# A mixture-of-experts loop: units of 64 slots for a pair of experts, one branch per pair, half of the sums kept in PSUM

## Chip, cores, metric

One core of one Trainium2 chip runs the whole program. The metric is the device time of one execution in microseconds (us); lower is better. Profiles are single executions recorded by the hardware profiler; times of runs are taken without it.

## What is computed

Two layers of a backbone over 512 tokens of width 1024. Each layer has a mixer (latent attention and a convolution in the first, a gated MLP in the second) and then a mixture of experts. The change is in the mixture alone. Cut to it, the reference reads:

```python
def hier_moe(h, w_group, b_group, w_router, b_router, w_gate, w_up, w_down):
    """Top-1 expert group (weight = group softmax prob), then top-2 experts within it."""
    ...
    out = jnp.zeros_like(t)
    for e in range(N_EXPERTS):                      # 32 experts, each 1024 -> 256 -> 1024
        he = (jax.nn.silu(t @ w_gate[e]) * (t @ w_up[e])) @ w_down[e]
        out = out + dense_w[:, e:e + 1] * he        # at most two experts of a token weigh more than 0
    return out.reshape(shp)
...
        h2 = modulate(rms_norm(x, norm2_g[l]), sh2, sc2)
        x = x + g2 * hier_moe(h2, *moe_args)
```

512 tokens with two experts each make 1024 rows for 32 experts, 32 on average. By the reference on its inputs the counts (expert p, expert p + 16) are, for p = 0 to 15:

| layer | counts |
|---|---|
| 0 | (27,35) (26,33) (24,32) (24,34) (17,11) (17,50) (20,19) (15,38) (50,29) (40,20) (36,50) (27,32) (69,42) (42,17) (39,28) (49,32) |
| 1 | (8,10) (39,7) (14,13) (20,2) (33,4) (16,6) (43,9) (23,7) (23,23) (20,103) (14,86) (8,103) (13,69) (42,82) (14,44) (30,96) |

## The kernel before

The kernel sorts the 1024 rows by expert on the chip. `Route` (lines 120 to 292) works out each row's rank within its expert, the experts' counts and where each expert's rows start. The rows of the normed activations are gathered in that order and turned, so that `m.xs` holds them with the channels on the partitions; this row stage also runs the first pair's unit beside it (tables `AUX` and `FIRST` say behind which block of rows what is issued).

`experts` then loops over 16 pairs: step j takes p = 0, 8, 1, 9, ..., 7, 15, that is the experts p and p + 16. A pair has six weight tiles of 1 MB, four with gate and up projections and two with down projections, 96 a layer; they are loaded in that order by SP's queue. About 14 are on their way before the loop, and `st.emit(6, j)` behind pair j's work issues six more.

The common unit holds up to 64 tokens of both experts. `gate_up` (L357) makes 32 matmuls of 512 columns, each with 64 columns of the array for one of the two experts; `act` multiplies silu(gate) by up (ACT L362, DVE L363); `turn` transposes (L370) and copies (ACT L371); `down` (L430) makes 16 matmuls of 512 into two banks. `weighed` multiplies by the token's weight and the layer's gain (DVE L419) and splits the product into a high part (ACT L420) and the rest (DVE L421), since the sums that follow run in a format that rounds; L388 and L389 build the one-hot matrix that says which row of x each slot belongs to. Those sums are sixteen matmuls L400, for four tiles of tokens, two halves of the width, high and rest. Each finished half is added to x at once, six by DVE (L413) and two by ACT and POOL (L410, L411).

`first(j + 1)` runs the next pair's gates and the sums of the pair that is due, between gates and transposes. It stands in both sides of a branch `few` (L623): where no expert of the pair has more than 64 tokens, `first` follows. Otherwise a second pass `again` follows (L451 gates, L459 down) for 64 slots of the expert with more (the `If` at L597 picks which). Behind it a branch `both` (L639) skips the part for pairs in which both experts have more than 64, or one more than 128; that part has a loop with a count in a register (L610). On these inputs it is never entered. Branches of `few` and `both` have a hint (L480, L482) that TensorE's queue issues ahead of them, from the count in a register.

Engines follow their own queues, and the order in each is the order of the code. Waits between them are semaphores.

Of the kernel before, what the change touches and what calls it, by code (L numbers as in the profile page):

```python
# [17 lines left out]
P = 128  # L18
# [3 lines left out]
SLOT = 64  # L22

# [93 lines left out]
class Route:  # L117
# [37 lines left out]
    def end(self, res):  # L155
# [23 lines left out]
        R0 = k.work.tile([P, 8, 64], BF16, name="R0", tag="w2", bufs=NW2)  # L179
# [6 lines left out]
        v.tensor_tensor(R0, io(8, 64), fb[:, 0][:, :, None].to_broadcast([P, 8, 64]), op=OP.is_equal)  # L186
        for q in range(8):
            for e in range(2):
                nc.tensor.matmul(p0[64 * e:64 * e + 64, 0:2], R0[:, q], B0[:, q, e], start=(q == 0), stop=(q == 7))
# [12 lines left out]
        with nc.allow_low_precision(reason="whole numbers under 512"):  # L202
            v.tensor_reduce(res.g0, p0[:, 0:2], axis=AX.X, op=OP.add)
# [10 lines left out]
        pin(v.tensor_copy(it[:, 0], ro[:, 0]))  # L214
# [8 lines left out]
    def starts(self, res):  # L223

        k, cc = self.k, self.cc
        v = k.nc.vector
        cm = k.small.tile([P, 16], F32, name="cm", tag="cm")
        for r in range(8):
            v.tensor_scalar(res.start[:, r], cc[:, 32:64], float(SLOT * r), 1024.0 - SLOT, op0=OP.add, op1=OP.min)
        v.tensor_tensor(cm, cc[:, 0:16], cc[:, 16:32], op=OP.max)  # L230
        v.tensor_copy(res.cnt[:, 0, :], cm)
        res.most = k.work.tile([P, 1], I32, name="most", tag="most")
        v.tensor_reduce(res.most, cm, axis=AX.X, op=OP.max)
        v.tensor_scalar(cc[:, 0:32], cc[:, 0:32], float(SLOT), None, op0=OP.is_gt)
        v.scalar_tensor_tensor(res.cnt[:, 2, :], cc[:, 16:32], 2.0, cc[:, 0:16], op0=OP.mult, op1=OP.add)
        v.tensor_scalar(cc[:, 0:16], cm, 2.0 * SLOT, None, op0=OP.is_gt)
        v.scalar_tensor_tensor(res.cnt[:, 3, :], res.cnt[:, 2, :], 3.0, cc[:, 0:16], op0=OP.is_equal, op1=OP.max)
        v.tensor_scalar(cm, cm, float(SLOT - 1), None, op0=OP.add)
        v.tensor_copy(res.cnt[:, 1, :], cm)
        v.tensor_scalar(res.cnt[:, 1, :], res.cnt[:, 1, :], 6, None, op0=OP.arith_shift_right)  # L240

        d = k.small.tile([P, 2, 16], F32, name="d", tag="rd")
        v.tensor_scalar(d[:, 0], res.cnt[:, 2, :], 2.0, None, op0=OP.is_equal)
        v.tensor_tensor(d[:, 1], res.start[:, 1, 16:32], res.start[:, 1, 0:16], op=OP.subtract)
        v.tensor_tensor(d[:, 1], d[:, 1], d[:, 0], op=OP.mult)
        v.tensor_tensor(res.second, d[:, 1], res.start[:, 1, 0:16], op=OP.add)
# [27 lines left out]
    def columns(self, r):  # L274
# [5 lines left out]
        if r:  # L280
            f = k.small.tile([P, 8], F32, name="fr", tag="fr")
            v.tensor_scalar(f, self.ft[:, 3], -32.0 * r, None, op0=OP.add)
# [51 lines left out]
def moe_bufs(k):  # L334

    m = K()
    ps = [k.psum.tile([P, 512], F32, name=f"mps{i}", tag=f"mps{i}", bufs=1) for i in range(8)]
    m.pg, m.ph, m.py, m.po = ps[0], ps[1], ps[2:4], ps[4:8]
    m.xT = k.work.tile([P, 8, P], F32, name="xT", tag="xT")
    m.mix = k.work.tile([P, D], F32, name="mix", tag="mix")  # L340
    m.xr = m.mix[:, 0:512].rearrange("p (c s) -> p c s", c=8)
    m.sg, m.h = m.mix[:, 512:768], m.mix[:, 768:1024]
    m.row = [k.work.tile([P, D], F32, name=f"row{i}", tag=f"y{i}") for i in range(2)]
    m.g2 = k.work.tile([P, D], F32, name="g2", tag="g2")
    m.hT = m.sg.rearrange("p (f s) -> p f s", f=2)
    m.xs = [W(k, [P, 2, D], "xs") for _ in range(4)]
    m.ic = k.small.tile([P, 2], I32, name="ic", tag="ic")
    m.t4 = k.small.tile([P, NT], F32, name="t4", tag="t4")
    m.tw = k.small.tile([P, 2, 2], F32, name="tw", tag="tw")
# [3 lines left out]
def gate_up(k, m, st, p, cs):  # L353

    for c in cs:
        for h in range(2):
            k.nc.tensor.matmul(m.pg[64 * h:64 * h + 64, :], m.xT[:, c, 64 * h:64 * h + 64], st.gu(p, h, c), start=(c == 0), stop=(c == 7))  # L357


def act(k, m):  # L360

    k.nc.scalar.activation(m.sg, m.pg[:, 0:256], AF.Silu)  # L362
    k.nc.vector.tensor_tensor(m.h, m.sg, m.pg[:, 256:512], op=OP.mult)  # L363


def turn(k, m, n=P):

    nc = k.nc
    for f in range(2):
        nc.tensor.transpose(m.ph[:, f * P:f * P + n], m.h[0:n, f * P:(f + 1) * P], k.ident[0:n, 0:n])  # L370
    nc.scalar.copy(m.hT[:, :, 0:n], m.ph[:, 0:2 * P].rearrange("p (f s) -> p f s", f=2)[:, :, 0:n])  # L371


SIDE = [(0, 1), (2, 0)]
SIDE0 = ()


class Outs:
# [3 lines left out]
    def __init__(self, oh, y):  # L382
        self.oh, self.y = oh, y
        self.left = ()

    def where(self, k, m, tok):
        eng = k.nc.vector
        eng.tensor_scalar(m.t4, k.noff, tok, None, op0=OP.add)  # L388
        eng.tensor_tensor(self.oh.rearrange("p (i t) -> p i t", i=NT), k.iota[:, None, :].to_broadcast([P, NT, P]),  # L389
                                m.t4[:, :, None].to_broadcast([P, NT, P]), op=OP.is_equal)  # L390

    def add(self, k, m, X, tiles):

        for i in tiles:
            for n in range(2):
                self.add_half(k, m, X, i, n)

    def sum_half(self, k, po, i, n, start=True, stop=True):
        for y in self.y:
            k.nc.tensor.matmul(po, self.oh[:, i * P:i * P + P], y[:, 512 * n:512 * n + 512],  # L400
                               start=start and y is self.y[0], stop=stop and y is self.y[-1])

    def add_half(self, k, m, X, i, n, side=SIDE):
        c = slice(512 * n, 512 * n + 512)
        po = m.po[(2 * i + n) % 4]
        if (i, n) in self.left:
            m.one.sum_half(k, po, i, n, stop=False)
        self.sum_half(k, po, i, n, (i, n) not in self.left)
        if (i, n) in side:
            k.nc.scalar.copy(m.tmp, po)  # L410
            k.nc.gpsimd.tensor_tensor(X[i][:, c], X[i][:, c], m.tmp, op=OP.add)  # L411
            return
        k.nc.vector.tensor_tensor(X[i][:, c], X[i][:, c], po, op=OP.add)  # L413


def weigh(k, m, py, w, s, c, hi, lo):

    nc = k.nc
    nc.vector.scalar_tensor_tensor(py[s], py[s], w[s], m.g2[s, c], op0=OP.mult, op1=OP.mult)  # L419
    nc.scalar.copy(hi, py[s])  # L420
    return lambda: nc.vector.tensor_tensor(lo, py[s], hi.bitcast(F32), op=OP.subtract)  # L421


def down(k, m, st, p):

    nc = k.nc
    for n in range(2):
        for f in range(2):
            for h in range(2):
                nc.tensor.matmul(m.py[n][64 * h:64 * h + 64, :], m.hT[:, f, 64 * h:64 * h + 64],  # L430
                                 st.dn(p, h, f)[:, 512 * n:512 * n + 512], start=(f == 0), stop=(f == 1))


def weighed(k, m, w, tok):

    m.one.where(k, m, tok)
    parts = []
    for n in range(2):
        c = slice(512 * n, 512 * n + 512)
        parts.append(weigh(k, m, m.py[n], w, slice(0, P), c, *(y[:, c] for y in m.one.y)))  # L440
    for low in parts:
        low()


def again(k, m, st, p, h, w, tok, fill):

    nc = k.nc
    a, b = slice(0, 64), slice(64, P)
    for c in range(8):
        for q, s in enumerate((a, b)):  # L450
            nc.tensor.matmul(m.ph[s, 256:512], m.xr[:, c], st.gu(p, h, c)[:, 256 * q:256 * q + 256], start=(c == 0), stop=(c == 7))  # L451
    nc.scalar.activation(m.sg[a], m.ph[a, 256:512], AF.Silu)
    nc.vector.tensor_tensor(m.h[a], m.sg[a], m.ph[b, 256:512], op=OP.mult)
    fill(0)
    turn(k, m, 64)
    fill(1)
    for f in range(2):
        for q, s in enumerate((a, b)):
            nc.tensor.matmul(m.py[1][s, :], m.hT[:, f, 0:64], st.dn(p, h, f)[:, 512 * q:512 * q + 512], start=(f == 0), stop=(f == 1))  # L459
    m.two.where(k, m, tok)  # L460
    parts = []
    for q, (s, o) in enumerate(((a, b), (b, a))):
        c = slice(512 * q, 512 * q + 512)
# [1290 lines left out]
```

## Time and profile before

| | us |
|---|---|
| runs, median of 3 | 1421.14 (1418.04 to 1421.16) |
| profiled execution | 1433.02 |
| its span, first to last instruction | 1431.2 |
| first loop over pairs (layer 0) | 242.3 |
| second loop over pairs (layer 1) | 297.8 |

Busy over the span: TensorE 1288.0 us (90%), its weight loads 835.3, DVE 850.7, ACT 558.8, POOL 319.0. The mean granted TensorE clock is 0.951 of full speed. The terms: PE is TensorE, PEld its weight loads, PEq and PEldq their sequencers, DVE, ACT, POOL and SP the others. A row of the chain or of a timeline begins with the start and the length in us. "x32" is a count of instructions. "[1.99 <-PEq L480]" is idle time ahead of the row and what ended it.

### The profile page before, as it was taken

The page shows a single profiled execution, that of the slowest core. Times are in us where ns is not written, and L with a number is a line of the kernel's source. Part 1 is how long each engine was busy: PE and PEld are TensorE (multiplying, and loading weights), DVE is VectorE, ACT ScalarE, POOL GpSimd, SP SyncE. Part 2 cuts the span into 40 slices and gives each one's busy share as a digit, 9 for nine tenths or more (in the row PEclk, how much of TensorE's full clock was granted, in tenths as well). Part 3 has the DMA queues.
Part 4 walks back from the last instruction along what each step waited for, and adds up shares of the span by engine and source line. Part 5 has one row for each costly group of instructions (what it writes and reads, how often), then busy time and mean ns, then how long its engine had stood idle before and what let it go on. Part 6 is the DMA issues. An engine that isn't in the chain of part 4 may idle for free. (4 is left out here: it accounts for less than half of the span.)

```text
span 1431.2 us, 20527 instructions
## 1 busy us (share of the span) xinstructions
PE 1288.0 (90%) x7174; PEld 835.3 (58%) x7174; DVE 850.7 (59%) x1730; ACT 558.8 (39%) x1315; POOL 319.0 (22%) x289
## 2 busy tenths in 40 slices
PE   5999878899996989989969999999995999999997
PEld 3678754454774444444458898997873444444443
DVE  2334687889667546564684455676347566555554
ACT  3244544476444424333352233344324433332331
POOL 0033454587102112121230001220002022111210
PEclk9999988899997999999989999999997999999998
DMA  9411044726546789989856354353367687877771
GB/s 360 156 32 44 17 167 135 293 72 221 221 166 248 287 345 412 413 348 387 354 181 224 123 203 159 133 196 133 122 253 272 261 359 310 344 293 291 297 306 61
DMA packets 54570, 329.12 MB, mean 230 GB/s; under 512 B 8030, under 2 KB 8286, under 8 KB 19634
## 3 DMA queue, kind: packets, MB, share of 16 engines
q1 hardware_dynamic: 48658, 306.29, 55.3%
q0 software_dynamic: 5664, 19.93, 4.3%
q8 instruction: 106, 1.74, 0.5%
q14 instruction: 142, 1.16, 0.2%
HBM read 317.77 MB, written 8.43 MB: 228 GB/s over the span
## 5 line engine op out<-in xcount | busy, mean ns | idle before, releaser
L357 PE MATMUL mps<-w,xT 128*64 128x512 f32 x1024 | 245.2, 632 | 27.6 <-PEq L480 10.1
L357 PEld LDWEIGHTS mps<-w,xT 128*64 128x64 f32 x1024 | 90.3, 145 | 175.9 <-issue 171.0
L411 POOL TENSOR_TENSOR X<-X,tmp 128x512 f32<-128x512 f32 x72 | 92.9, 1291 | 443.1 <-ACT tmp L410 386.4
L700 PE MATMUL ps_c<-wch,hxh 128*128 128x256 f32 x512 | 147.6, 288 | 2.0 <-ACT hxh L706 2.0
L702 PE MATMUL ps_c<-wch,hxl 128*128 128x256 f32 x512 | 145.8, 285 | 1.5 <-DVE rm_m L98 0.9
L701 PE MATMUL ps_c<-wcl,hxh 128*128 128x256 f32 x512 | 146.0, 286 | 0.0
L400 PE MATMUL mps<-oy,ooh 128*128 128x512 f32 x512 | 138.8, 408 | 1.7 <-ACTq L623 1.7
L413 DVE TENSOR_TENSOR X<-X,mps 128x512 f32<-128x512 f32 x206 | 132.8, 683 | 10.8 <-PE mps L400 9.0
L363 DVE TENSOR_TENSOR mix<-mix,mps 128x256 f32<-128x256 f32 x32 | 13.5, 421 | 185.6 <-ACT mix L362 185.6
L430 PE MATMUL mps<-w,mix 128*64 128x512 f32 x512 | 116.9, 598 | 0.0
L400 PEld LDWEIGHTS mps<-oy,ooh 128*128 128x128 f32 x512 | 91.4, 189 | 43.0 <-issue 22.2
L891 POOL TENSOR_TENSOR acc<-acc,ctp 128x497 f32<-128x497 f32 (+14 forms) x71 | 101.8, 1462 | 32.9 <-ACT ctp L890 32.9
L700 PEld LDWEIGHTS ps_c<-wch,hxh 128*128 128x128 f32 x512 | 98.9, 193 | 7.8 <-issue 4.2
L701 PEld LDWEIGHTS ps_c<-wcl,hxh 128*128 128x128 f32 x512 | 99.0, 193 | 4.2 <-issue 3.4
L702 PEld LDWEIGHTS ps_c<-wch,hxl 128*128 128x128 f32 x512 | 98.8, 193 | 4.5 <-issue 1.7
L362 ACT ACTIVATE mix<-mps 128x256 f32<-128x256 f32 x32 | 12.3, 384 | 202.5 <-PE mps L357 199.7
L430 PEld LDWEIGHTS mps<-w,mix 128*64 128x64 f32 x512 | 33.9, 136 | 66.1 <-issue 55.2
L700 PE MATMUL ps_o<-woh,yTh 128*128 128x512 f32 x160 | 64.7, 406 | 2.1 <-ACT v L1333 1.2
L420 ACT CAST oy<-mps 128x512 fp32r<-128x512 f32 x64 | 37.2, 585 | 75.0 <-DVE mps L419 75.0
L706 POOL TENSOR_TENSOR vs<-v,vs 128x512 fp32r<-128x512 f32 x16 | 23.0, 1440 | 182.1 <-ACT vs L706 174.7
L701 PE MATMUL ps_o<-wol,yTh 128*128 128x512 f32 x160 | 63.3, 396 | 0.0
L702 PE MATMUL ps_o<-woh,yTl 128*128 128x512 f32 x160 | 62.9, 394 | 0.0
(412 smaller groups left out, 2527.7 us busy)
## 6 DMA issues: line engine op xcount, KB each, us to landing
w<-in_w_gu_dram SPq DMA_DIRECT2D x128, 1024.0 KB
w<-in_w_down_dram SPq DMA_DIRECT2D x64, 1024.0 KB
wada<-in_w_ada_dram SPq DMA_DIRECT2D x48, 1024.0 KB
wc<-in_c_w_in_dram SPq DMA_DIRECT2D x16, 1024.0 KB
wo<-in_c_w_out_dram SPq DMA_DIRECT2D x8, 1024.0 KB
X<-in_x_dram SPq DMA_DIRECT2D x4, 1024.0 KB
wo<-in_ab_w_out_dram SPq DMA_DIRECT2D x4, 1024.0 KB
h2d<-row POOLq DMA_DIRECT2D x16, 256.0 KB, 5.2
```

Of the source, the lines that this page charges most:

```text
L357: k.nc.tensor.matmul(m.pg[64 * h:64 * h + 64, :], m.xT[:, c, 64 * h:64 * h + 64], st.gu(p, h, c), start=(c == 0), stop=(c == 7))
L363: k.nc.vector.tensor_tensor(m.h, m.sg, m.pg[:, 256:512], op=OP.mult)
L400: k.nc.tensor.matmul(po, self.oh[:, i * P:i * P + P], y[:, 512 * n:512 * n + 512], start=start and y is self.y[0], stop=stop and y is self ...
L411: k.nc.gpsimd.tensor_tensor(X[i][:, c], X[i][:, c], m.tmp, op=OP.add)
L413: k.nc.vector.tensor_tensor(X[i][:, c], X[i][:, c], po, op=OP.add)
L420: nc.scalar.copy(hi, py[s])
L430: nc.tensor.matmul(m.py[n][64 * h:64 * h + 64, :], m.hT[:, f, 64 * h:64 * h + 64], st.dn(p, h, f)[:, 512 * n:512 * n + 512], start=(f == 0 ...
L700: k.nc.tensor.matmul(out, lh, rh, start=start, stop=False)
L701: k.nc.tensor.matmul(out, lh, rl, start=False, stop=False)
L702: k.nc.tensor.matmul(out, ll, rh, start=False, stop=stop)
L706: for i in (k.nc.scalar.copy(hi, src), (eng or k.nc.vector).tensor_tensor(lo, src, hi.bitcast(F32), op=OP.subtract)):
L891: nc.gpsimd.tensor_tensor(d, d, tp, op=OP.add)
```

## The change

A unit now has 64 slots: either 32 tokens of each expert of a pair, or 64 of one. `Unit` (new) has both kinds. For a pair, the array's columns are cut into four groups of 32: expert, and half of the 512 columns (gate or up; left or right half of the down product). For one expert they are two groups of 64, as in the second pass before. Gates, transposes and down products share two banks (`m.pg`, `m.py`).

The sums are eight matmuls, since the high part and the rest lie in one tile `y`, one above the other. The left half of the width (n = 0) is summed in four banks `m.acc` over the whole layer and added to x at its end. The right half goes to two banks and is added by DVE at once, as before; no sum goes by ACT and POOL.

The branches: after a pair's unit, `some(extra)` skips to the join where no expert of the pair has over 32 tokens. Otherwise a unit of one expert follows, and `some(more)` skips what is for still more; that goes through `further`, a loop `For_i` over the number of windows left, which sets the tokens and weights of its window by eight small matmuls. `weigh` of a unit is issued behind the join, or ahead of the next unit of the same pair. The next pair's unit is written once, behind the join, and not in both sides of a branch.

In the row stage the first unit has half of the columns, `Route.heads` makes 32 small matmuls for the tables of the 32-token heads, and the conditional block at L563 is gone. The diff, cut:

```diff
+HEAD = 32
...
+    def heads(self, pt):
+
+        for q in range(8):
+            s = self.S[:, q // 4, q % 4].rearrange("p (a b s) -> p a b s", a=2, b=2)[:, 0, 1]
+            for a in range(4):
+                self.k.nc.tensor.matmul(pt[HEAD * a:HEAD * a + HEAD], s, self.C[q // 4][:, q % 4, :, 0:32], start=(q == 0), stop=(q == 7))
...
-    m.pg, m.ph, m.py, m.po = ps[0], ps[1], ps[2:4], ps[4:8]
...
+    m.pg = ps[7][:, 0:256]
+    m.py, m.po, m.acc = ps[0], ps[1:3], ps[3:7]
...
+            self.parts = [(slice(HEAD * q, HEAD * q + HEAD), slice(HEAD * (q % 2), HEAD * (q % 2) + HEAD), q % 2, q // 2) for q in range(4)]
+            self.x = m.xT
+        else:
+            self.parts = [(s, A, h, q) for q, s in enumerate((A, B))]
+            self.x = m.xr
+
+    def gates(self, cs=range(8)):
+        for c in cs:
+            for r, s, h, q in self.parts:
+                self.k.nc.tensor.matmul(self.m.pg[r], self.x[:, c, s], self.st.gu(self.p, h, c)[:, 256 * q:256 * q + 256], start=(c == 0), stop=(c == 7))
...
+def weigh(k, m):
+
+    v, y, c = k.nc.vector, m.y, [slice(0, 512), slice(512, D)]
+    v.scalar_tensor_tensor(m.py, m.py, m.tw[:, 1:2], m.g2h, op0=OP.mult, op1=OP.mult)
+    for s, cs in zip((A, B), c):
+        k.nc.scalar.copy(y[s, cs], m.py[s])
+    v.tensor_scalar(m.oh, m.seq, m.tw[:, 0:1], None, op0=OP.is_equal)
+    for s, o, cs in zip((A, B), (B, A), c):
+        v.tensor_tensor(y[o, cs], m.py[s], y[s, cs].bitcast(F32), op=OP.subtract)
...
+    def run(u, tw, turned=None):
+
+        u.gates()
+        u.act()
+        for i in range(4):
+            scatter(k, m, m.acc[i], i, 0, False, False)
+        u.turn()
+        for f in range(2):
+            for i in range(2):
+                scatter(k, m, m.po[i], 2 * f + i, 1, True, True)
+                add(m.po[i], 2 * f + i, 1)
+            if turned and f == 0:
+                turned()
+            u.down([f])
+        nc.vector.tensor_copy(m.tw, tw)
+
+    def further(u, h, p, n):
...
+        with tc.For_i(0, n, 1):
+            v.tensor_scalar(m.ic, m.at, float(-HEAD), 1024.0 - SLOT, op0=OP.add, op1=OP.min)
+            window(m.xr, m.ic[0:1])
+            weigh(k, m)
...
+            for q in range(8):
+                nc.tensor.matmul(m.pg[:, 0:2], rt.S[:, q // 4, q % 4], m.cw[:, q], start=(q == 0), stop=(q == 7))
+            v.tensor_copy(m.pw, m.pg[:, 0:2])
+            run(u, m.pw)
...
-        few = tc.If(count(0, p, 512) <= SLOT, preferred_fallthrough_block=False, label=f"few{l}_{j}")
-        with few as more:
-            if not last:
-                first(j + 1, m.one)
...
+        kind = value(0, p, 3)
+        with some(f"extra{l}_{j}", kind):
+            ahead_of(f"more{l}_{j}", 3, p, 16)
+            weigh(k, m)
+            with tc.If(kind == 2) as other:
+                run(us[1], res.tw1[:, :, p + 16])
             with other.Else():
...
+                run(us[0], res.tw1[:, :, p])
+            with some(f"more{l}_{j}", value(3, p, 16)):
+                for h in range(2):
+                    n = value(1 + h, p, 8)
+                    with tc.If(n > 0):
+                        further(us[h], h, p, n)
+        weigh(k, m)
         st.emit(6, j)
```

On TensorE, before, a second pass ends so: the last down matmuls, the jump out of the `If`, the load of the count and the branch `both`, then sums that were left (`oy` and `ooh` are the weighed rows and the one-hot matrix).

```order
L459 MATMUL mps_3750<-w,mix 64x512 x3
L597 UNCONDITIONAL_BRANCH
L473 TENSOR_LOAD cnt
L639 COMPARE_AND_BRANCH
L400 MATMUL mps_3752<-oy_4103,ooh 128x512
L400 MATMUL mps_3752<-oy_4104,ooh 128x512
```

On TensorE, after, a pair's unit ends so: the last down matmuls (32 rows a group), the load of the count and the branch `extra`, the hint for `more`, the `If` on which expert, then a unit of one expert.

```order
L411 MATMUL mps_3746<-w,mix 32x512 x4
L434 TENSOR_LOAD cnt
L444 COMPARE_AND_BRANCH
L434 TENSOR_LOAD cnt [waits DVE_49]
L439 REGISTER_ALU
L1691 BRANCH_PREFETCH_HINT
L596 COMPARE_AND_BRANCH
L392 MATMUL mps_3753<-w,xr 64x256 x16
```

No sum stands behind the branch any more, and a further unit is reached over two branches.

On TensorE, after, the same unit of one expert ends, and `further` follows (L603 the `If` around it, L570 its loop, L579 the small matmuls):

```order
L411 MATMUL mps_3746<-w,mix 64x512 x2
L596 UNCONDITIONAL_BRANCH
L434 TENSOR_LOAD cnt
L444 COMPARE_AND_BRANCH
L434 TENSOR_LOAD cnt
L603 COMPARE_AND_BRANCH
L570 COMPARE_AND_BRANCH
L570 UNCONDITIONAL_BRANCH [waits PE_49]
L570 UNCONDITIONAL_BRANCH [waits barrier_Pool_Activation_PE_DVE_SP_release]
L1691 BRANCH_PREFETCH_HINT
L579 MATMUL mps_3753<-cw,S 128x2 [waits DVE_49]
L579 MATMUL mps_3753<-cw,S 128x2 x7
```

Between two units there stand five branches, a barrier of all engines, and small matmuls that wait for DVE. A second barrier, at the loop's end, waits for the transfer queues too.

On DVE, before, the weighing stands ahead of the branch `few`:

```order
L388 TENSOR_SCALAR t_3765<-ct,tok_102 128x4 [waits DVE_49]
L389 TENSOR_TENSOR ooh<-ct,t_3765 128x512 [waits DVE_49]
L419 SCALAR_TENSOR_TENSOR mps_3749<-mps_3749,w_103,g_3759 128x512 [waits DMASW2_49]
L419 SCALAR_TENSOR_TENSOR mps_3750<-mps_3750,w_103,g_3759 128x512
L421 TENSOR_TENSOR oy_4104<-mps_3749,oy_4103 128x512 [waits DMASW1_49,Activation_49]
L421 TENSOR_TENSOR oy_4104<-mps_3750,oy_4103 128x512 [waits Activation_49]
L473 TENSOR_LOAD cnt
L623 COMPARE_AND_BRANCH
```

On DVE, after, the branch `extra` stands ahead of it (L563 copies the unit's tokens and weights):

```order
L563 COPY tw<-tw_103 128x2 [waits DVE_49]
L434 TENSOR_LOAD cnt
L444 COMPARE_AND_BRANCH
L416 SCALAR_TENSOR_TENSOR mps_3746<-mps_3746,tw,g_3759 128x512 [waits DVE_49,PE_49]
L419 TENSOR_SCALAR oh<-g_3759,tw 128x512
L421 TENSOR_TENSOR y<-mps_3746,y 64x512 [waits DVE_49,Activation_49]
L421 TENSOR_TENSOR y<-mps_3746,y 64x512
L596 COMPARE_AND_BRANCH
```

The load of the count and the branch moved ahead of the weighing, which has one product where it had two.

## Rows read from the trace of the kernel before

**Rows 1.** Busy time by stretch: row stage, layer 0, layer 1, one full stretch.
```profile
core 0: us, PE busy (x) PEld busy (x) DVE busy (x) ACT busy (x) POOL busy (x), PEclk, DMA share, GB/s
444.00:474.60 30.60, 25.52 (x138) 14.05 (x138) 21.03 (x82) 18.30 (x50) 7.61 (x9) 0.89 0.58 191
474.60:716.90 242.30, 234.53 (x1040) 108.57 (x1040) 136.98 (x208) 85.56 (x275) 41.16 (x32) 0.97 0.92 372
1120.30:1418.10 297.80, 279.90 (x1296) 132.89 (x1296) 163.11 (x253) 98.68 (x302) 51.78 (x40) 0.97 0.74 292
540.00:600.00 60.00, 60.00 (x274) 26.38 (x272) 36.66 (x55) 22.29 (x74) 11.12 (x9) 1.00 1.01 412
```
**Rows 2.** The chain that ended last, a pair without a second pass.
```profile
1377.66 6.87 PE mps L357 x32
...
1388.67 3.58 PE mps L430 x16
```
**Rows 3.** The same chain, the second pass of the last pair.
```profile
1408.60 3.67 PE mps L451 x32
1412.28 2.07 PE mps L400 x8
1414.35 0.26 PE mps L370 x2
1414.61 1.59 PE mps L400 x6
1416.20 1.89 PE mps L459 x8
```
**Rows 4.** TensorE's timeline, another stage: matmuls with 32 columns each.
```profile
203.99 1.07 PE L720 MATMUL ps_ada<-wada,sc 128*32 128x512 f32 x8
```
**Rows 5.** TensorE's waits over the span: total us, times, longest us.
```profile
PE mps L357 <- PEq L480: 10.1, 6, 2.3
PE mps L357 <- ACT oy L420: 8.6, 4, 2.2
```
**Rows 6.** TensorE's branches: duration in ns, least, median, greatest; first and last start.
```profile
L639 PEldq COMPARE_BRANCH  x10: 194/280/2891, 1172.2 to 1343.3; - x10
...
L623 PEldq COMPARE_BRANCH  x39: 82/363/6427, 473.4 to 1403.6; - x39
```
**Rows 7.** Busy time by stretch, columns as in rows 1: gates behind two joins.
```profile
1175.30:1182.50 7.20, 7.15 (x33) 2.44 (x34) 2.15 (x3) 0.84 (x2) 0.00 (x0) 1.00 0.96 374
1215.00:1224.00 9.00, 8.92 (x33) 2.94 (x34) 1.69 (x3) 0.62 (x2) 0.00 (x0) 0.81 0.96 391
```
**Rows 8.** The chain that ended last, weighing of the last second pass.
```profile
1418.12 0.76 DVE mps L419
...
1418.90 0.59 ACT oS L420
...
1420.32 0.59 ACT oS L420
...
1420.93 0.70 DVE oS L421
```
**Rows 9.** SP's semaphore steps at the program's end, as in rows 6.
```profile
L1750 SPq EVENT_SEMAPHORE  x14: 17/28/28, 1427.8 to 1431.1; - x14
```
**Rows 10.** DVE's timeline: a small instruction.
```profile
1211.40 0.22 DVE L388 TENSOR_SCALAR t<-ct,tok 128x4 f32<-128x4 f32 x1
```
**Rows 11.** TensorE's timeline in the row stage of layer 0.
```profile
446.65 5.74 PE L357 MATMUL mps<-w,xT 128*64 128x512 f32 x16
...
457.95 3.65 PE L357 MATMUL mps<-w,xT 128*64 128x512 f32 x16
...
462.47 1.95 PE L292 MATMUL mps<-C,S 128*128 128x128 f32 x16
...
467.55 3.65 PE L430 MATMUL mps<-w,mix 128*64 128x512 f32 x16
```

More of the change, by code (lines that the diff above doesn't have):

```diff
@@ L225, in starts @@
         k, cc = self.k, self.cc
[L226 to L233, printed above, removed]
@@ L242, in starts @@
[L242 to L246, printed above, removed]
+        v, sm = k.nc.vector, k.small
+        n, e = sm.tile([P, 4, 16], F32, name="cm", tag="cm"), lambda h: slice(16 * h, 16 * h + 16)
@@ L337, in moe_bufs @@
     ps = [k.psum.tile([P, 512], F32, name=f"mps{i}", tag=f"mps{i}", bufs=1) for i in range(8)]
[L338 to L342 removed]
+    m.pg = ps[7][:, 0:256]
+    m.py, m.po, m.acc = ps[0], ps[1:3], ps[3:7]
+    m.last = m.po + [m.py, m.acc[0]]
@@ L366, in turn @@
[L366 to L413, printed above, removed]
@@ L434, in weighed @@
[L434 to L463, printed above, removed]
-        parts.append(weigh(k, m, m.py[1], w, s, c, m.two.y[0][s, c], m.two.y[0][o, c]))
-    for low in parts:
-        low()
@@ L484, in window, with ahead_of, some @@
-    def window(x, at, act=False):
+                              skip_runtime_bounds_check_because="numbers of windows of at most 512 tokens", **kw)
+    def ahead_of(label, row, p, most):
+        tc.mark_branch_hint_location(label, hint=value(row, p, most, engines=(PE,)) > 0, engines=(PE,))
+    @contextmanager
+    def some(label, v):
+        with tc.If(v <= 0, preferred_fallthrough_block=False, label=label) as g:
+            pass
+        with g.Else():
+            yield
+    def window(x, at, n=SLOT, act=True):
@@ L492, in windows, with heads, seconds @@
-    def windows(j):
+            (nc.scalar.copy if act else nc.vector.tensor_copy)(x[:, 2 * c:2 * c + 2], m.xs[c][:, :, bass.ds(o, n)])
+    def heads(j):
         p = pair(j)
         for h in range(2):
-            window(m.xT[:, :, 64 * h:64 * h + 64], res.start[0:1, 0, p + 16 * h:p + 16 * h + 1], True)
+            e = p + 16 * h
+            window(m.xT[:, :, HEAD * h:HEAD * h + HEAD], res.start[0:1, 0, e:e + 1], HEAD)
+    def seconds(j):
+        p = pair(j)
+        window(m.xr, res.second[0:1, p:p + 1])
@@ L570, in experts @@
-    m.one = Outs(tile([P, 512], "oh"), [tile([P, D], f"y{i}") for i in range(2)])
-    m.two = Outs(tile([P, 512], "C0"), [tile([P, D], "S")])
-    m.tmp = k.work.tile([P, 512], F32, name="tmp", tag="C1")
-    def first(j, due):
-        ahead_of(f"few{l}_{j}", 0, pair(j), 512, SLOT)
-        gate_up(k, m, st, pair(j), range(8))
-        act(k, m)
-        due.add(k, m, X, (0, 1))
-        turn(k, m)
-        if j < 15:
-            windows(j + 1)
-        due.add(k, m, X, (2, 3))
-    ends = [(n, i) for n in range(2) for i in range(4)]
+                ahead_of(f"extra{l}_0", 0, pair(0), 3)
@@ L586, in experts @@
     for j in range(16):
         p = pair(j)
-        last = j == 15
-        window(m.xr, res.second[0:1, p:p + 1], True)
-        ahead_of(f"few{l}_{j}", 0, p, 512, SLOT)
+        seconds(j)
         if j:
-            down(k, m, st, p)
-        weighed(k, m, res.w0[:, p:p + 1], res.tok0[:, p:p + 1])
-        one = lambda r, e: (res.w[:, r, e:e + 1], res.tok[:, r, e:e + 1])
-        def second(fill):
-            with tc.If(count(2, p, 3) == 2) as other:
-                again(k, m, st, p, 1, *one(1, p + 16), fill)
-            with other.Else():
-                again(k, m, st, p, 0, *one(1, p), fill)
@@ L1468 @@
 ROWAHEAD = 0
-FILL = [[(0, 0), (0, 1), (1, 0)], [(1, 1), (2, 0)]]
-LEFT = [(i, n) for i in range(4) for n in range(2) if (i, n) not in FILL[0] + FILL[1]]
 COLWAIT = 3
```

282 lines of the change are left out of this document (129 added, 153 removed).

## The prediction

> **What bounds the kernel now.** I read the table by stage first. The two loops over the pairs of experts take 242.3 and 297.8 us, 540.1 of the span of 1431.2, and TensorE is busy for 234.5 and 279.9 of it [rows 1]. The weights' loads are the other candidate: 96 tiles of 1 MB a layer, and the stretch in which the transfer engines are always busy shows 412 GB/s, so 2.55 us a tile and 245 us a layer; the loops show a share of 0.92 and 0.74 [rows 1]. So TensorE sets the pace, with the loads close behind in layer 0. Then the chain that ended last: a pair without a second pass is nothing but TensorE, 6.87 for the gates, 3.58 for the down products [rows 2] and sixteen sums between them, about 14.6 in all. A second pass costs 3.67 + 2.07 + 0.26 + 1.59 + 1.89 [rows 3]. What TensorE loses, 25.7 us over both loops, lies at branches [rows 5].
>
> **What is counted.** How many tokens each expert has follows from the reference on its inputs. Before, a pair has a second pass where an expert has over 64 tokens: one in layer 0, six in layer 1. Now the common unit holds 32 + 32 slots. In layer 0, 12 of 16 pairs need more than that, in layer 1 ten; of these 22, five need still more: (36, 50) and (69, 42) in layer 0, (20, 103), (8, 103) and (42, 82) in layer 1. Units: 16 + 14 and 16 + 13, 59; the first of each layer runs in the row stage, so 57 run in the loops.
>
> **The unit.** A unit of one expert has the matmuls of today's second pass: 32 of 256 columns, 3.67; two transposes, 0.26; eight of 512, 1.89 [rows 3]. A unit of a pair has the same columns in four groups of 32. Four groups of 32 columns run at once in this kernel: eight matmuls of 512 took 1.07, as two at 0.5 each would [rows 4]. So I give both units the same price. The sums become 8 where the common pass had 16, 0.261 each (2.07 and 1.59 for 14, [rows 3]), 2.09. Unit: 3.67 + 2.09 + 0.26 + 1.89 = 7.91; 57 units, **450.9**. The weighing hides: one DVE product, two ACT copies, one subtraction follow each other, 0.76 + 0.59 + 0.59 + 0.70 = 2.6 [rows 8], with some 0.5 for the branch ahead of them, behind the next gates of 3.67. If that cover were gone, it would be up to 3.1 a unit; I take 0.
>
> **The joins.** Today six joins after a second pass hold TensorE 10.1 us in all, 1.7 each, and four where the `few` branch jumps the other way than the hint had it 8.6 [rows 5]. The branch itself lasts 0.28 in the middle case and 2.89 in the worst [rows 6]. Now: ten pairs without a further unit, one jump each, 1.2 (between 0.3 and 2.2), **12.0**. Fifteen joins behind a second unit with another unit to come, 1.7 each, **25.5** (4 to 43). Entering the 22 further units, 0.2 each, a little under the middle branch of 0.28 [rows 6] (0 to 1.2), **4.4**. After about half of today's joins the granted clock falls: 0.81 over one next pair's gates against 1.00 over another's, where the stretch was 9.0 us for the matmuls that otherwise take 7.2 [rows 7], 1.7 us. Half of fifteen, **12.8** (0 to 25).
>
> **The five loops.** A third window goes through `further`, a loop with a count in a register. Its beginning and its end make every engine wait for every other and for every transfer queue; today's program has that nowhere in the loops (the like loop of before is never entered). Nothing in the trace shows its price, so I build it up. The loads of its counts and branches around it, like a join and a bit: 1.9. A barrier at the entry, 1.0, and one with the queues at the end, 1.6: together 2.6, under the 3.3 in which the program itself closes, from the first to the last of its semaphore steps [rows 9]. Between them nothing overlaps: the weighing, 2.6 [rows 8], four small DVE instructions at 0.22 each [rows 10], eight tiny matmuls into the gates' bank and a copy, 0.9 (the two transposes took 0.26, [rows 3]), 4.4 in all. Back to the next unit 1.9. Sum 10.8, and two stretches at the lower clock, 3.4 [rows 7]: 14.2. Five, **71**. The bounds lie far apart: a join's price, 2.55, from below; three jumps at the worst of today's, 6.43 [rows 6], with 5.7 for the rest, 25, from above. I take the middle, since the serial parts have rows of their own.
> Then the loads. They are queued two to three pairs ahead, and the barrier waits for those on their way. Carried forward pair by pair (6 tiles of 2.55 arrive against 9.1 us of a pair with one unit and 19 of one with two, 14 tiles ahead at the start), some 8.5, 2.2, 6, 2.2 and 0 us are outstanding at the five: **19** (0 to 40).
>
> **Other engines.** On DVE the weighing now stands behind the branch's register load; queued behind it are the next unit's product of the gates and the sums, which come 3.7 us later. Its additions fall from six a unit to four, so DVE has room. ACT and POOL lose the two sums that went by them. Nobody waits for SP but the loads, which are issued after the join as today.
>
> **The row stage and the ends.** Gates of the first unit are 16 + 16 matmuls of half the columns in effect: 5.74 and 3.65 become 2.9 and 1.85; down products 3.65 becomes 1.9 [rows 11]: 6.4 less. The new `heads` adds 32 small matmuls; sixteen matmuls of 128 columns take 1.95 [rows 11], so 1.0 if four at a time share the array and 3.9 if not; I take 2.5. That is 3.9 less a layer, **7.9** for both (0 to 11: TensorE has 5 us of idle there, [rows 1]). At the ends of the layers all eight sums stand behind the last weighing; I add **2** (-3 to 8).
>
> **The sum.** 450.9 + 12.0 + 25.5 + 4.4 + 12.8 + 71 + 19 = 595.6 where 540.1 stood: +55.5; less 7.9, plus 2: +49.6. The profiled execution took 1433.0, 11.9 more than the median of the runs, 1421.1; so 1482.6 under the profiler and **1470** in the runs. The units take 89 us less than the loops of before; the joins and the `further` loops cost more than that.
>
> **Rivals.**
> A. Faster. The loops are cheap: the jumps fall through and the barriers find everything landed, so that a loop costs a join's 2.55. Then 71 + 19 becomes 12.8, 77 less: **1393**. For it speak that the branches of today mostly cost 0.28 [rows 6] and the middle share of the transfers in layer 1, 0.74 [rows 1]; against it, that the serial chain alone is 4.4. It decides below 41 us for all five with their loads, some 8 each.
> B. About equal. Loops of 6 with 8 us of loads: 38 in place of 90, 52 less: **1418**.
> C. Much slower. Every taken jump stalls like today's bad ones: 25 joins at 2.2 + 1.7 instead of the 50.3 that I count, 47 more, and four jumps in each of five loops at 2.2, 44 more: **1561**. For it: the jump in `few` has a worst case of 6.43, in `both` 2.89 [rows 6]. Against it: the middle ones.
> [...]
> D. The change doesn't do what it says: four groups of 32 columns with 256 columns each don't run at once, and 28 of the units cost 3.6 more: +101, **1571**. Against it [rows 4].
>
> **Chances.** The forecast with loops of 6 to 22, 1430 to 1510, 0.54; A 0.23; B 0.07; C 0.12; D 0.04. The range from 1385 to 1540 takes in the forecast, B and most of A, and leaves out most of C and D. A measurement of this kernel can tell about 0.3%, 4 us, from no change: faster is A, 0.23; the same is B, 0.07; slower is the rest, 0.70.
>
> **What would show it.** TensorE's time from one unit's first gate matmul to the next one's in a pair with one unit: 7.9 plus about 1.2 (D: 11.5). Gaps ahead of a pair's gates behind a second unit: 1.7, in C 2.2 and more at every one. In the five pairs with a loop, some 22 us from the second unit's last matmul to the next pair's first, of which 7.9 is TensorE's unit and the rest idle; in A it is 10.5. The granted clock below 1.00 in the stretches behind joins. The mean share of transfers in the loops falls. I would be wrong above all in the loops, whose price has no row; next in the joins, if the hints come early enough to make each of them 0.3 (35 less); and in the weighing, if it doesn't stay behind the gates: 57 units turn each 0.5 us into 28.

## The result and the profile after

The changed kernel takes 1510.64 us, median of 4 runs (1506.78 to 1513.95), against 1420.69 us: 1.0636 times as long, 95% interval 1.0607 to 1.0666. The forecast was 1470 in a range from 1385 to 1540: slower, as it said, but by 90 us where it had 49.

The table by stretch of the changed kernel, with the columns of [rows 1]: first the row stage of layer 0, then the loops over pairs of layer 0 and layer 1.

```profile
core 0: us, PE busy (x) PEld busy (x) DVE busy (x) ACT busy (x) POOL busy (x), PEclk, DMA share, GB/s
435.80:464.80 29.00, 22.19 (x246) 14.66 (x246) 22.41 (x86) 18.38 (x54) 9.39 (x11) 0.91 0.58 201
464.80:776.03 311.23, 263.62 (x2082) 135.21 (x2082) 163.37 (x304) 87.18 (x298) 0.00 (x0) 0.93 0.73 290
1181.60:1496.70 315.10, 265.24 (x2049) 135.88 (x2048) 159.48 (x304) 86.36 (x299) 0.00 (x0) 0.90 0.69 276
```

The loops take 626.3 us and had 540.1 [rows 1]: 86.2 more, 69 of them in layer 0, where 14 further units stand against one second pass. TensorE's idle time in the loops went from 25.7 to 97.5 us, its busy time from 514.4 to 528.9. The row stages are 3.2 us shorter, the layers' ends 5.5 longer: 88.5. The stretches ahead of the two row stages, whose code is unchanged, took 10.0 us less in this profiled execution (6.9 and 3.1), which is how its 1511.49 stands only 78.5 above the 1433.02 of before.

What a pair looks like now. TensorE's timeline: one unit of a pair, then one of an expert (its first row only, and its last), then the next pair.

```profile
476.30 3.66 PE L392 MATMUL mps<-w,xT 128*32 128x256 f32 x64 [1.38 <-PEq L434]
479.89 1.20 PE L426 MATMUL mps<-y,oh 128*128 128x512 f32 x4
481.01 0.33 PE L404 MATMUL mps<-ct,mix 64*128 64x64 f32 x2
481.27 0.73 PE L426 MATMUL mps<-y,oh 128*128 128x512 f32 x2
481.94 1.06 PE L411 MATMUL mps<-w,mix 128*32 128x512 f32 x8
482.93 0.74 PE L426 MATMUL mps<-y,oh 128*128 128x512 f32 x2
483.60 1.06 PE L411 MATMUL mps<-w,mix 128*32 128x512 f32 x8
484.73 3.67 PE L392 MATMUL mps<-w,xr 128*64 128x256 f32 x32
...
492.05 1.08 PE L411 MATMUL mps<-w,mix 128*64 128x512 f32 x4
494.44 0.85 PE L392 MATMUL mps<-w,xT 128*32 128x256 f32 x12 [1.31 <-PEq L434]
```

Four groups of 32 columns do run at once: 64 matmuls take 3.66, as the 32 with two groups do. A unit takes 8.36 us. Nothing idles inside it, and going on to the further unit costs nothing. Going to the next pair costs 1.3.

What TensorE waits for, over the span (total us, times, longest us); these answer to [rows 5].

```profile
PE mps L579 <- DVE cw L576: 29.8, 5, 6.2
PE mps L392 <- DVE oh L419: 24.7, 8, 4.6
PE mps L392 <- PEq L434: 22.6, 17, 1.4
...
PE mps L392 <- ACTq L444: 3.1, 1, 3.1
...
PE mps L392 <- DVEq L444: 2.6, 1, 2.6
```

The first row is the five third windows, the others are joins. The row that names DVE's `oh` has seven long joins in it, at which TensorE's own branch took 1.9 to 4.4 us; the last two rows are joins at which TensorE waited for another engine's jump (below, under joins and hints). I added up the loops' 57 units and the gaps ahead of them from TensorE's rows. The clock's part is the excess over 3.67 us of gates in stretches with a granted clock under 1.00, the loads' part the idle time inside gates and the excess at a clock of 1.00:

| part of the two loops | predicted | measured |
|---|---|---|
| 57 units | 450.9 | 477.7 (8.38 each) |
| joins and entries | 41.9 | 50.6 (25 gaps) |
| third windows with the join behind, without unit and the gates' clock | 54 | 56.0 (49.2, and 6.8 in five gaps) |
| lower clock | 29.8 | 31.3 |
| waiting for weight loads | 19 | 10.3 |
| sum | 595.6 | 625.9 |

### The profile page after: what moved, and what is told of

It is laid out like the page before. It is cut to its first block, busy times and chain, and to the rows that moved or that the text cites. A ratio compares the mean times of both kernels' runs of the same rounds, so it can differ in the third digit from the quotient of the medians.

```text
span 1509.7 us, 25483 instructions
## 1 busy us (share of the span) xinstructions
PE 1288.5 (85%) x9158; PEld 863.0 (57%) x9158; DVE 875.1 (58%) x1875; ACT 548.7 (36%) x1343; POOL 230.7 (15%) x221
## 5 line engine op out<-in xcount | busy, mean ns | idle before, releaser
L392 PE MATMUL mps<-w,xT 128*32 128x256 f32 x2048 | 141.7, 430 | 65.4 <-DVE oh L419 24.7
L426 PE MATMUL mps<-y,oh 128*128 128x512 f32 x472 | 159.5, 441 | 7.0 <-DVE y L421 7.0
L392 PEld LDWEIGHTS mps<-w,xT 128*32 128x32 f32 x2048 | 81.5, 123 | 135.8 <-issue 107.4
L418 ACT CAST y<-mps 64x512 fp32r<-64x512 f32 x118 | 68.3, 579 | 199.9 <-DVE mps L416 193.9
L426 PEld LDWEIGHTS mps<-y,oh 128*128 128x128 f32 x472 | 81.5, 192 | 90.5 <-DVE X L547 47.1
L411 PE MATMUL mps<-w,mix 128*32 128x512 f32 (+1 forms) x728 | 126.0, 608 | 0.3 <-issue 0.3
L421 DVE TENSOR_TENSOR y<-mps,y 64x512 fp32r<-64x512 f32 x118 | 81.3, 689 | 59.8 <-ACT y L418 58.1
L392 PE MATMUL mps<-w,xr 128*64 128x256 f32 x864 | 112.1, 417 | 2.5 <-DVE pw L580 1.7
L392 PEld LDWEIGHTS mps<-w,xr 128*64 128x64 f32 x864 | 68.9, 151 | 52.6 <-issue 30.2
L416 DVE SCALAR_TENSOR_TENSOR mps<-mps,tw,g 128x512 f32<-128x512 f32 x59 | 44.7, 758 | 32.9 <-PEq L444 15.3
```

Of the source, the lines that this page charges most:

```text
L392: self.k.nc.tensor.matmul(self.m.pg[r], self.x[:, c, s], self.st.gu(self.p, h, c)[:, 256 * q:256 * q + 256], start=(c == 0), stop=(c == 7))
L411: self.k.nc.tensor.matmul(self.m.py[r], self.m.hT[:, f, s], self.st.dn(self.p, h, f)[:, 512 * q:512 * q + 512], start=(f == 0), stop=(f == 1))
L416: v.scalar_tensor_tensor(m.py, m.py, m.tw[:, 1:2], m.g2h, op0=OP.mult, op1=OP.mult)
L418: k.nc.scalar.copy(y[s, cs], m.py[s])
L421: v.tensor_tensor(y[o, cs], m.py[s], y[s, cs].bitcast(F32), op=OP.subtract)
L426: k.nc.tensor.matmul(ps, m.oh[:, i * P:i * P + P], m.y[:, 512 * n:512 * n + 512], start=start, stop=stop)
```

## Experiments

Times are medians, 4 runs of each kernel and 7 of the kernel before, if not said otherwise. The ratio is to the kernel before; the changed kernel's is 1.0636.

### Third windows: the loop, the chain, the whole

First the loop itself (`e1_straight`).

```diff
-        with tc.For_i(0, n, 1):
+        if True:
```

> The third window is written straight, without a loop: on these inputs each of the five pairs has exactly one third window, so the work is the same, but the barriers of all engines at the loop's beginning and end are gone. Theory: the gap of 5.8 to 6.2 us ahead of the small matmuls is the serial chain over DVE and ACT, not the barrier, and stays; so do the small matmuls (3.5 us) and the join behind (1.3). What goes is that SP stands in the loop for 15 to 18 us and issues no weight load, so that later gates wait for loads (some 13 us in all); 5 to 15 us less, about 1500 us. Rival: the barriers are the price, as the prediction had them (2.6 us and 1.9 of loads and branches a loop): the gap falls to about 3 us, 15 to 25 us less, about 1490.

1505.99 us, ratio 1.0584 (1.0505 to 1.0663): 5 us less, and the intervals overlap. The gap ahead of the small matmuls stays, 5.5 to 6.2. The barrier was not the price. But my own reason for a gain fell too: loads are still waited for (6 us inside gates and one gap of 9.6 on a load, against 10.3). What went is the join behind a third window: without a loop TensorE falls through into the next pair, five gaps of nothing where 1.3 stood.

The changed kernel's third window, TensorE's timeline and then DVE's, shows where the 5.9 is.

```profile
558.35 1.08 PE L411 MATMUL mps<-w,mix 128*64 128x512 f32 x4
565.26 3.54 PE L579 MATMUL mps<-cw,S 128*128 128x2 f32 x16 [5.84 <-DVE cw L576]
569.15 6.09 PE L392 MATMUL mps<-w,xr 128*64 128x256 f32 x32 [0.34 <-DVE pw L580]
...
581.28 1.93 PE L392 MATMUL mps<-w,xT 128*32 128x256 f32 x32 [1.32 <-PEq L434]
```

```profile
560.79 0.75 DVE L416 SCALAR_TENSOR_TENSOR mps<-mps,tw,g 128x512 f32<-128x512 f32 x1
561.45 0.48 DVE L419 TENSOR_SCALAR oh<-g,tw 128x512 fp32r<-128x512 f32 x1
563.40 1.39 DVE L421 TENSOR_TENSOR y<-mps,y 64x512 fp32r<-64x512 f32 x2 [1.48 <-ACT y L418]
564.81 0.15 DVE L574 TENSOR_SCALAR at<-at 128x1 f32<-128x1 f32 x1
564.88 0.16 DVE L575 SCALAR_TENSOR_TENSOR cw<-fr,ct 128x8 f32<-128x8 f32 x1
564.96 0.16 DVE L576 SCALAR_TENSOR_TENSOR cw<-fr,wc 128x8 f32<-128x8 f32 x1
```

The matrix `cw`, for which TensorE waits, is made by two instructions of 0.16, queued on DVE behind 4 us of weighing. And behind the loop's end the next gates wait 1.32, as behind any join: TensorE passed the closing barrier 0.4 us after its last matmul in all five, and no load held it there. `e12_early` moves the weighing behind the small matmuls; `e13_both` is that without the loop.

```diff
             window(m.xr, m.ic[0:1])
-            weigh(k, m)
...
+            weigh(k, m)
             v.tensor_copy(m.pw, m.pg[:, 0:2])
             run(u, m.pw)
```

> In a third window the small DVE instructions and the eight small matmuls are issued ahead of the weighing, not behind it. Theory: the 5.9 us ahead of the small matmuls are mostly the weighing (2.6 to 3.3 us), which then lies beside them (3.5 us): the gap falls to 2.7 to 3.3, five times about 2.9 less, 14 us less, about 1497. Rival: the gap is branches, register loads and the barrier: it stays above 5 us and the time within 4 us of 1511.

> The third window written straight, without a loop, and the small matmuls ahead of the weighing. Theory: the two gains add, 5 and 14 us: about 1492, still 70 us above the kernel before, since joins, units and second units of layer 0 are as they were. Rival: without the barrier the weighing was hidden already: 1503 or more.

`e12_early`: 1495.1 us, ratio 1.0534 (1.0497 to 1.0571). `e13_both`: 1487.89, ratio 1.0459 (1.0414 to 1.0505). Both times are as the theory had them. The timeline of `e12_early`:

```profile
563.54 1.92 PE L578 MATMUL mps<-cw,S 128*128 128x2 f32 x16 [1.94 <-DVE cw L575]
567.32 6.23 PE L392 MATMUL mps<-w,xr 128*64 128x256 f32 x32 [1.86 <-DVE pw L580]
```

The gaps and small matmuls of the five windows fall from 49.2 to 29.2 us, with up to 1.9 moved into the wait for `pw`, which now stands on DVE behind the weighing. 5.6 of it are the small matmuls themselves, which behind the shorter gap have a higher granted clock (1.00 in two windows, 0.60 to 0.78 in three). The stretches of the two rows above, first of the changed kernel and then of `e12_early`, with the columns of [rows 1]:

```profile
565.26:568.80 3.54, 3.54 (x16) 3.46 (x16) 0.06 (x1) 0.00 (x0) 0.00 (x0) 0.50 0.00 0
```

```profile
563.54:565.46 1.92, 1.92 (x16) 1.83 (x16) 1.11 (x3) 1.86 (x6) 0.00 (x0) 1.00 0.55 226
```

In the changed kernel all five are at 0.50, so some 8 us of what the table has under third windows are the clock too.

Last, all of it: `e4_nothird` leaves the third windows out.

```diff
-            ahead_of(f"more{l}_{j}", 3, p, 16)
...
-            with some(f"more{l}_{j}", value(3, p, 16)):
-                for h in range(2):
-                    n = value(1 + h, p, 8)
-                    with tc.If(n > 0):
-                        further(us[h], h, p, n)
```

> The third windows are left out (the five pairs that have one miss it in the output, so the time is that of 54 units with 30 joins). Theory: a third window costs 5.9 of chain, 3.5 of small matmuls, 0.3, a unit of 8.4 and 2.2 of half clock, 20.4 us, and the loads held in SP cost 13 more in all: 115 us less, about 1396. Rival, the prediction's prices: 7.9 + 14.2 each and 19 of loads, 130 less, about 1381. Should it be under 85 less, the cost that is laid to the loops lies elsewhere.

1395.28 us, ratio 0.9811 (0.9743 to 0.9879): 115 less than the changed kernel. One further unit, 8.4 of it, is missing beside the third windows: x lacks their rows after layer 0, and in layer 1 the pair with the counts (33,4) has one unit where it should have two. Behind its down product the next pair follows:

```profile
1252.11 1.07 PE L411 MATMUL mps<-w,mix 128*32 128x512 f32 x8
1254.50 0.63 PE L392 MATMUL mps<-w,xT 128*32 128x256 f32 x6 [1.32 <-DVE mps L416]
```

The trace of the changed kernel gives the five windows by themselves: the units' own matmuls 42 (8.38 each), gaps and small matmuls 49.2, joins behind them 6.8, lower clock over their gates 11.1, together 109. So these five are more than the whole loss of 90 us. That the 115 meets the expectation is partly luck: a unit is missing, and the long jumps moved. In this kernel most joins fall through, but behind six of the now eleven pairs with one unit there is a gap of 4.6 to 7.6.

### Joins and hints

`e2_hint` issues a pair's hint behind the unit's gates, `e7_twice` there as well as at the join (and the one for `more` twice too), `e6_nohint` not at all.

```diff
         u.gates()
+        if hint:
+            hint()
...
-            ahead_of(f"extra{l}_{j}", 0, p, 3)
-            run(Unit(k, m, st, p), res.tw0[:, :, p], (lambda: heads(j + 1)) if j < 15 else None)
+            run(Unit(k, m, st, p), res.tw0[:, :, p], (lambda: heads(j + 1)) if j < 15 else None,
+                lambda: ahead_of(f"extra{l}_{j}", 0, p, 3))
```

> The hint for the branch of a pair is issued behind the gates of the pair's unit, where TensorE's sequencer runs ahead of the array, and not at the join. Theory: a join is a row of register instructions of TensorE's sequencer, of which the load for the hint, its arithmetic and the hint are 0.5 to 0.6 us and lie on the path: each of the 30 joins is 0.55 us shorter, 1.3 becomes 0.75, 16 us less, about 1494; a little more if the clock holds better behind shorter gaps. Rival: the jump's code fetch and the semaphore steps set the join's price, and the load lies beside them: joins stay at 1.3, within 4 us of 1511.

> The hints are issued where they were and once more behind the unit's gates, 4.2 us ahead of the jump. With the hint only there, nine of the ten pairs with one unit had a long branch, where it was three with the hint 8.4 us ahead. Theory: the lead counts, and a second hint for the same target changes nothing: 9 or fewer joins over 2 us, gaps of 55 to 65 us in all, within 6 us of 1511. Rival: the latest hint counts, its fetch begins anew: over 20 joins above 2 us, gaps above 90 us, about 1555.

> The branch hints of the pair loops are left out. Theory: what makes a join long is that the code it jumps to has to be fetched, and a hint hides that only if it is early enough; without one each of the 25 taken jumps takes 2.5 to 4.5 us, and the hint's own load (0.55 us a join) is gone: gaps ahead of a pair's gates add up to 90 to 110 us where they were 57, the clock costs some more, about 1550. Rival: the hints do nothing but cost their load: 16 us less, about 1495.

`e2_hint`: 1521.26 us, ratio 1.069 (1.0619 to 1.076), not the 16 us less. `e7_twice`: 1517.97, 1.0657 (1.058 to 1.0734). `e6_nohint`: 1552.24, 1.0897 (1.0837 to 1.0957), the time expected, with gaps of 86 us where 90 to 110 were expected: eight of the fifteen joins behind a second unit stayed short without a hint. TensorE's waits at joins, first of `e2_hint`, then of `e6_nohint`:

```profile
PE mps L392 <- PEq L444: 51.6, 21, 5.9
```

```profile
PE mps L392 <- PEq L444: 77.2, 23, 6.2
```

The gaps ahead of a pair's gates, and how many are over 2 us, by kind of pair (the leads are those of the sequencer's records from hint to branch; the expectations had them as 8.4 and 4.2):

| kernel | hint for a pair with one unit | sum of 30 gaps | one unit (10) | second unit (15) |
|---|---|---|---|---|
| changed kernel | 7.5 to 10.3 us ahead, once 5.4 | 57.4 | 3 | 6 |
| `e2_hint` | 4.6 to 4.9 us ahead, once 5.4 | 62.8 | 9 | 5 |
| `e7_twice` | both | 70.0 | 5 | 5 |
| `e6_nohint` | none | 86.4 | 10 | 7 |

The pair at 5.4 us is the first of layer 1. Its hint stands in the row stage and was not moved; it held in the changed kernel (gap 1.29) and in `e2_hint` (0.73).

Half of the theory stands: where the jump is short, the join fell from 1.3 to 0.71 in `e2_hint`, so the hint's load is on the path, 0.6. But the moved hints, all nine with a lead under 5 us, failed, with gaps of 3.0 to 5.9, while pairs with a second unit, whose hint hadn't moved, did as before. A second hint changes the picture for some pairs, but neither as the theory (55 to 65 us of gaps) nor as its rival (over 90) had it. A branch row of the changed kernel answers to [rows 6]:

```profile
L444 PEldq COMPARE_BRANCH  x81: 68/191/4356, 463.9 to 1497.1; - x81
```

Without a hint, in `e6_nohint`, the gap is 4.5 to 6.2 us in nine of the ten pairs with one unit, whose jump passes the code of four units. That a fetch of that code fills this time, as my theory for `e6_nohint` had it, is inferred from these gaps and from the name of the hint's instruction; no row shown here has the fetch itself. In the changed kernel TensorE's branch took 0.4 us behind each of the four hints with 9.5 us and more of lead. But behind nine hints with 7.5 to 8.1 us it took 1.2 to 4.4, and behind others with the same lead 0.4 to 0.5; what tells these apart, no run settled.

Two of the nine joins over 2 us are not, or not only, TensorE's own jump. The hints of the pair loops are issued for TensorE alone, and the other engines jump too. At the join of 3.1 us TensorE's branch took 0.47, but ACT passed its own branch at 1264.9 and made its next step at 1269.1, with nothing to do between:

```profile
L444 ACTq EVENT_SEMAPHORE  x2: 17/17/17, 1269.1 to 1269.2; - x2
L444 ACTq COMPARE_BRANCH  x1: 58/58/58, 1264.9 to 1264.9; - x1
```

The gates started at 1269.21. At the join of 2.6 us, DVE took 2.9 over its jump, beside 1.7 of TensorE's. No run gave these engines a hint.

### The unit's order

`e3_order` puts two sums ahead of the four and the down product in one piece. `e10_together` and `e11_split` have no additions of the right half; the first has all eight sums together, the second the change's order.

```diff
         u.gates()
-        u.act()
+        u.silu()
+        for i in range(2):
+            scatter(k, m, m.po[i], i, 1, True, True)
+        add(m.po[0], 0, 1)
+        u.times()
+        add(m.po[1], 1, 1)
         for i in range(4):
             scatter(k, m, m.acc[i], i, 0, False, False)
         u.turn()
...
+        for i in range(2):
+            scatter(k, m, m.po[i], 2 + i, 1, True, True)
+            add(m.po[i], 2 + i, 1)
...
+        u.down()
```

> Within a unit, two of the sums of the right half come before the four of the left half, and the two halves of the down product stand together at the end: three changes between kinds of matmul fewer. Theory: the unit takes 8.38 us and not 7.91 because each change from sums to down product and back costs TensorE 0.1 to 0.15 us; it becomes 7.95 to 8.05, 57 units, 19 to 25 us less, about 1489. Rival: the matmuls themselves cost more than the rows of before had it (0.27 to 0.30 a sum), the order does nothing, or DVE's additions now hold the second pair of sums: within 5 us of 1511 or slower.

> A measurement of TensorE's order alone: the additions of the right half to x are left out (the output lacks them), and all eight sums stand together between gates and transposes, the down product in one piece behind. Theory: a unit's matmuls cost what the rows of before had, 3.6 + 2.1 + 0.26 + 1.9, and the rest of 8.38 is changes between kinds: 7.9 to 8.0 us a unit. Rival: the matmuls themselves are dearer: 8.3 or more.

> The counterpart: the same additions are left out, but the order is that of the change (four sums, transposes, two sums, half of the down product, two sums, the other half). Theory: 8.38 us a unit as with the additions, since DVE is no limit there. Rival: the second pair of sums waits for DVE in the change: the unit falls to 8.0 here as well.

`e3_order`: 1519.81 us, ratio 1.0652 (1.057 to 1.0734): no gain, its rival. The other two took 1483.18 and 1477.04 us in one run each. Without the additions the pair (33,4) of layer 1 has one unit here too, so a unit's rows are compared and not these times. Of `e10_together`, TensorE's timeline:

```profile
493.45 2.12 PE L426 MATMUL mps<-y,oh 128*128 128x512 f32 x8
495.50 0.33 PE L404 MATMUL mps<-ct,mix 64*128 64x64 f32 x2
496.19 1.92 PE L411 MATMUL mps<-w,mix 128*32 128x512 f32 x16 [0.35 <-ACT mix L405]
```

Together the eight sums take 2.12, as before [rows 3], and the down product 1.92. Split up as in the change, the sums come to 1.20 + 0.73 + 0.74 and the down product to 1.06 + 1.06. These lengths overlap where one group ends and the next begins; from first start to last end, the unit of `e10_together` without its wait of 0.35 is 0.46 us shorter than that of `e11_split`. So the theory of the changes between kinds is right about the price, 0.46 us for the three changes more, and wrong about the gain: sums between transposes and down product cover ACT's copy of the turned values, and where they are moved away, TensorE waits 0.35 for it. The unit comes to 8.26 and not to 8.0; in `e11_split` it stays at 8.38. In `e3_order` the second pair of sums took 0.96 where two take 0.73; what held it, no row here shows. The joins of that run came to 65 us, so its unit alone doesn't explain its time.

### Weighing and PSUM

`e8_weigh` issues the weighing at the unit's end, `e9_nopsum` adds the left half in each unit as well.

```diff
         nc.vector.tensor_copy(m.tw, tw)
+        weigh(k, m)
...
-        weigh(k, m)
         st.emit(6, j)
```

```diff
-            scatter(k, m, m.acc[i], i, 0, False, False)
+            scatter(k, m, m.acc[i], i, 0, True, True)
+            add(m.acc[i], i, 0)
```

> A unit's weighing is issued at the end of the unit, ahead of the branch, and no longer behind the join. Theory: it lies behind the next gates either way: within 5 us of 1511. Rival: the branch's register loads on DVE and ACT come ahead of the weighing today and make sums wait: it begins 0.5 us earlier at each join and the loops' chain of 5.9 us gets shorter by 2.6, 15 to 25 us less, about 1490.

> No sums are kept in PSUM: the left half too is added to x by DVE in each unit. Theory: DVE has 8 additions of 0.684, 2.6 of weighing and 0.6 more, 8.7 us of work and its gaps for a unit in which TensorE needs 8.4; a unit gets 0.5 to 1.5 us longer, 57 units, 30 to 85 us more, about 1565. Rival: DVE is busy 58% of the time and takes the additions beside the rest, as it took six of eight before: within 10 us of 1511.

`e8_weigh`: 1607.88 us, ratio 1.1296 (1.1228 to 1.1363). Neither of its theories: 97 more. All but one of the 30 joins are 3.8 us or longer, 129 us in all where they were 57, and the lower clock costs 64 us where it was 31. The profile puts the wait to ACT:

```profile
PE mps L392 <- ACT xr L455: 86.3, 23, 5.0
```

That copy makes the input of the next second unit, and the gates don't read it. What TensorE's first gate matmul waits for in the records is a count of DVE's, and DVE raises it for the skipped block when it passes the join itself. These are DVE's semaphore steps at one join (first and last start at the end), of `e8_weigh` and of the changed kernel; the gates start at 500.36 and 494.44.

```profile
L444 DVEq EVENT_SEMAPHORE  x2: 21/21/21, 500.2 to 500.3; - x2
```

```profile
L444 DVEq EVENT_SEMAPHORE  x2: 21/21/21, 493.3 to 493.4; - x2
```

In `e8_weigh` DVE has the weighing ahead of its jump and comes 3.7 us after TensorE's last matmul; in the change it comes 0.2 after it, and weighs behind the join beside the gates.

`e9_nopsum`: 1586.58 us, ratio 1.111 (1.1042 to 1.1178): 76 more, within the theory's range. The unit takes 9.9 us, and TensorE waits in each of the 57:

```profile
PE mps L426 <- DVE X L545: 59.6, 57, 1.1
```

So the two smaller parts of the change are worth 97 and 76 us to it. Undone, either would have made it slower still.

## Why the prediction came out as it did

**Direction.** Right, and by the mechanism forecast: the 57 units take 62 us less than the loops of before, and joins, third windows, clock and loads add 148. The third windows decide the sign: in the trace they come to 109 us where the whole change lost 88.5, and `e4_nothird`, which leaves their rows out, is 27 us faster than the kernel before, some 19 if the unit that it also lacks is added at 8.4.

**The unit** is the term that was mis-sized most, 7.91 for 8.38, 27 us in 57. I took each matmul's price from a stretch of its own kind and added no price for the changes between them, which the rows of [rows 3] show only once each. `e10_together` gives the old prices back.

**The joins** were 42 and are 51. The short ones were right (1.3 for 1.2). The step that failed is one price for every join of a kind: of these 25 gaps 16 are 1.3 to 1.5 and nine are 2.2 to 4.6. The fifteen behind a second unit come to 29.8 where I had 25.5, six of them long; the ten in pairs with one unit to 20.8 where I had 12.0, three of them long. Rival C had them all at 2.2. That the next unit is entered at no cost, I had at 4.4 us. And I priced TensorE's jump alone, where two of the nine were another engine's.

**The third windows** came to 56 for 54, from other parts than I gave, so that the sum is luck. I counted 2.6 us of barriers; `e1_straight` shows next to none on the path: without them the gap stays at 5.5 to 6.2. The eight small matmuls I took at 0.9 with their copy; they are 16 records and 3.5 us at a granted clock of 0.50. The weighing in series I had, and `e12_early` shows that it was there for its place in DVE's queue alone.

**The clock** was right in sum, 31 for 30, but not in its parts: ten joins cost 18.6 over the next gates where I had 12.8, the third windows' gates 11.1 where I had 17, the first gates of layer 0 1.7, and the small matmuls, which the 31 leaves out, some 8. The rows behind two joins, columns as in [rows 1], with gaps of 2.63 and 1.38 ahead of them:

```profile
600.60:606.00 5.40, 5.38 (x65) 3.38 (x66) 2.52 (x4) 2.06 (x6) 0.00 (x0) 0.68 0.97 401
476.30:480.00 3.70, 3.70 (x65) 2.46 (x66) 2.00 (x4) 2.06 (x6) 0.00 (x0) 1.00 0.82 319
```

**The loads** were 19 and are 10, in another place: no barrier held TensorE for them. They are missed by gates of later pairs, above all pairs with one unit, which take 9.7 us where six tiles take 15.3 at my estimate of 2.55 each. One row is enough to see it, a clock of 1.00 and a full share of transfers with TensorE busy for 4.3 of 5.1:

```profile
541.30:546.40 5.10, 4.32 (x65) 2.61 (x66) 1.78 (x4) 2.05 (x6) 0.00 (x0) 1.00 1.01 418
```

**The weighing at nothing** was right, but the cover was named by half: the next gates hide it only because the weighing stands behind the join. Ahead of the join, in `e8_weigh`, the same weighing holds the gates up: all but one of the 30 joins are 3.8 us or longer.

**Row stage and ends**: 3.2 less where I had 7.9, 5.5 more where I had 2. The eight sums behind the last weighing start 3.5 us after the last unit in both layers.

**A rival's sum.** D counted 28 units of a pair; the loops have 30, so that it should have stood at 108 us more and not 101. [rows 4] spoke against it, and the 3.66 us of a pair's gates rule it out.

No version made here that computes all rows beats the kernel before; the best of the changed kernel, `e13_both`, is 4.6% slower.

## What to carry to other kernels

Where branches cut a kernel into short units, price the changes as well as the work: here 0.15 us each between kinds of matmul, 1.3 to 4.6 at a join, and behind it the clock, 0.56 to 0.73 over the next gates at ten of the 25 joins. Put what an engine need not finish before a join behind it: in `e8_weigh` TensorE waited there for DVE's count and not only for its data, and the weighing ahead of the join cost 97 us. And count how often the rare path is taken: third windows in five of 32 pairs cost 109 us here, more than the 90 that the change lost.

## What was not expected of the hardware

Of nine hints 7.5 to 10.3 us ahead of the jump of a pair with one unit, two left TensorE a branch of 3.4 and 4.4 us and the others one of 1.2 or less; moved to under 5 us ahead, all nine left one of 2.3 to 6.2; one that stayed at 5.4 us held in both kernels. Without a hint the same ten jumps left gaps of 3.1 to 6.2. ACT, which has no hint, once took 4.2 us over a jump, and TensorE waited 3.1 for it. A join that waits for another engine's count cost 3.8 us where that engine had 3.7 us of work ahead of its jump. Sixteen matmul records of two columns took 3.5 us at a granted clock of 0.50 behind an idle stretch of 5.8, and 1.9 to 3.0 at 1.00 to 0.60 behind one of 2.
